# A hybrid attention/retention layer on one core: its modulation products in bursts of 16 k-tiles instead of 8, with half of their tiles in another pool

## The chip, the cores and the metric

The kernel runs on one core of a Trainium2 chip. The time is the device time of one execution in microseconds, as the median of several runs. The core has TensorE (PE for its matmuls, PEld for its weight loads), VectorE (DVE), ScalarE (ACT), GpSimd (POOL) and SyncE (SP), which issues most of the loads here.

## The reference, cut to what matters

One layer of a diffusion backbone: 256 latent tokens `x` and 256 context tokens `ctx`, width 4096, all in float32.

```python
mod = silu(c) @ ada_w + ada_b            # ada_w is 4096 x 12288
shift, scale, gate = split(mod, 3)
mod_c = silu(c_ctx) @ ada_w[:, :2*D] + ada_b[:2*D]
shift_c, scale_c = split(mod_c, 2)
h  = rms_norm(x, norm_w) * (1 + scale) + shift
hc = rms_norm(ctx, norm_w) * (1 + scale_c) + shift_c
proj = h @ w_in                          # 4096 x 14336; k and v of hc as well
...                                      # two groups of heads, gates
y = concat([o_d, o_r]) @ w_out
return x + gate * y
```

The change concerns the first lines: shift and scale of both token sets, that is two vectors (`c`, `c_ctx`) times the first 8192 columns of `ada_w`.

## The kernel before

The contraction of `h @ w_in` is cut into 32 k-tiles of 128 rows. A k-tile of `h` (its transposed tokens, 512 columns) can only be made when shift and scale of its 128 features are known, and these need all 4096 rows of the columns of `ada_w` that belong to it. So the kernel begins with a stage that alternates: the first `K1 = 20` k-tiles are worked off in chunks (`CHUNKS`: 1, 1, then nine times 2 k-tiles). For each chunk the adaLN products (class `Ada`) run over all 32 row tiles of `ada_w`, `finish` and `modulate` make the chunk's tiles `h`, and then six heads (`sheads`) multiply them with their columns of `w_in`: one `SUnit` a head, four row groups, three products each (a value is split in a high and a low part in `prep`), that is 24 matmuls of 512 columns where the chunk has two k-tiles. What is left of the 32 k-tiles is modulated later, on VectorE (`ada2_task`), beside other heads.

An adaLN product has a stationary operand of 32 columns, so four of them stand side by side in the array (`g = k % 4`); in float32 each is two passes, which the profile shows as two matmuls. `Ada.unit` runs one burst: `nk = 8` products, tied in order by `issue_after`, highest k first. A chunk has 32 products, so four bursts. `ada_to` calls `unit` so that a chunk's bursts are spread over the SUnits of the chunk before it (`LEAD`).

The tiles of `ada_w` have 4 KB a partition, 512 KB in all, loaded by two DMAs of 256 KB (`ada_load`, line 219). One holds two k-tiles of a chunk of width 2, or four of a chunk of width 1. They come from tag `adaw` with `ADAB = 6` buffers. `Ada.load` asks for the tiles of the next burst that is not asked for yet; it is called three times in the setup and once after each burst, so it stays three bursts ahead; a load waits until a buffer is free.

The pool `a4` has `SLOTS = 41` tiles of the same 4 KB a partition. It holds `x` and `ctx` at first (16), the transposed tokens `xr` (16, one for two k-tiles, free again when both are modulated), the tiles `h` (one a k-tile) and the sums of the heads `kvqg` (10 in this stage).

The weights of the heads go through `raw` (`RAWB = 3` buffers), are split on ACT (line 386) and DVE (line 387), four buffers each. Their DMAs (line 378) and those of `ada_w` are issued by SP, in one order: a DMA that has to wait holds those behind it. The order of the instructions on each engine, SP's issues among them, and the slots that tiles get, are fixed when the kernel is built, by a planner that goes by the order in the code and by its own estimate of when each thing is ready.

Of the kernel before, what the change touches and what calls it, by code (L numbers as in the profile page):

```python
# [10 lines left out]
F32 = mybir.dt.float32  # L11
# [7 lines left out]
P = 128  # L19
# [19 lines left out]
K1 = 20  # L39
# [4 lines left out]
ADAB = 6  # L44
# [38 lines left out]
def hybrid_kernel(es, tc, x, c, ctx, c_ctx, norm_w, ada_w, ada_b, w_in, q_norm_w, k_norm_w,  # L83
# [12 lines left out]
    a4 = es.enter_context(tc.tile_pool(name="a4", bufs=SLOTS, side="right"))  # L96
# [63 lines left out]
    adap = ada_cm.__enter__()  # L160
# [45 lines left out]

    ada_units = []
    for j, cn in enumerate(CHUNKS):
        nk = 8
        for k0 in range(0, KT, nk):  # L210
            ada_units.append((j, k0, nk))
    ada_end = [sum(1 for a in ada_units if a[0] <= j) for j in range(len(CHUNKS))]

    def ada_load(c0, cn, k0, name):

        n, m = cn * P, 4 // cn
        t = adap.tile([P, m, 2, n], F32, name=name, tag="adaw", bufs=ADAB)
        for s in range(2):
            nc.sync.dma_start(t[:, :, s], ada_w[k0 * P:(k0 + m) * P, s * D + c0 * P:s * D + c0 * P + n]  # L219
                              .rearrange("(k p) n -> p k n", p=P))  # L220
        return [t[:, k].rearrange("p s n -> p (s n)") for k in range(m)]

    class Ada:
# [5 lines left out]
        def load(self):  # L229

            p = self.pos + len(self.loaded)
            if p >= len(ada_units):
                return
            j, u0, nk = ada_units[p]
            tiles = []
            for k0 in range(u0, u0 + nk, 4 // CHUNKS[j]):
                tiles += ada_load(c0s[j], CHUNKS[j], k0, f"ada{j}_{k0}")
            self.loaded.append(tiles)
# [57 lines left out]
    def ada2_task():  # L296
# [4 lines left out]
        def load():  # L301
            if len(ahead) < len(work):
                j, k = work[len(ahead)]
                ahead.append(ada_load(c0s2[j], CHUNKS2[j], k, f"ada2_{j}_{k}")[0])
# [30 lines left out]
    ada = Ada()  # L335
    rbc = adap.tile([P, 512], F32, name="rbc")
    pr = aux_tile([P, 512], "pr")
    for half in range(2):
# [24 lines left out]
            nc.vector.tensor_scalar(dg, ident, rs[:, r:r + 1], None, op0=ALU.mult)  # L363
            nc.tensor.matmul(pr[:, rt * P:(rt + 1) * P], ones, dg, start=True, stop=True)
        ada.load()
    ada.load()
    nc.scalar.copy(rbc, pr)


# [720 lines left out]
```

## Time and profile before

| | |
|---|---|
| median of 3 runs | 2545.53 us (2541.44 to 2547.76) |
| the profiled execution | 2544.53 us |
| its span in the profile | 2542.7 us |
| PE busy | 2508.3 us of the span, mean granted clock 0.991 |
| moved by DMA | 563.70 MB |

The profile is of one execution; its own time is 1.8 us longer than the span. Times in its rows are from the start of the span. The profiled execution lies 1.0 us under the median of the runs.

### The profile page before, as it was taken

How to read it: one execution, taken by the hardware profiler on the slowest of the kernel's cores; microseconds unless marked ns; L12 is line 12 of the kernel's file. 1: busy time of each engine (PE TensorE's matmuls, PEld its weight loads, DVE VectorE, ACT ScalarE, POOL GpSimd, SP SyncE). 2: the span in 40 equal slices, each digit the busy share in tenths (PEclk: the TensorE clock that was granted, in tenths of full speed). 3: DMA queues.
4: the chain of work that ended last, by engine and by line, in shares of the span. 5: the costliest groups of instructions: out<-in, count | busy, mean ns of one | idle time of the engine just before them, and what ended most of it. 6: DMA issues, size and time to landing. Idle time of an engine off the chain costs nothing.

```text
span 2542.7 us, 36389 instructions
## 1 busy us (share of the span) xinstructions
PE 2508.3 (99%) x12634; PEld 2123.9 (84%) x12634; DVE 1726.4 (68%) x3026; ACT 992.2 (39%) x2017; POOL 44.6 (2%) x47
## 2 busy tenths in 40 slices
PE   7999999999999999999999999999999999999999
PEld 4566666888999997788888788899999999878887
DVE  5555555795897946777876887777777666655554
ACT  4222222222323233354445444554444444544443
POOL 0000000000000000000000000000000000000000
PEclk8999999999999999999999999999999999999999
DMA  9987978785686748766776676556666556676765
GB/s 315 291 284 243 292 230 292 244 269 176 198 274 192 252 105 278 235 219 196 239 241 202 201 238 227 185 178 199 198 207 203 169 152 189 197 238 207 229 208 175
DMA packets 497240, 563.70 MB, mean 222 GB/s; under 512 B 31696, under 2 KB 385296, under 8 KB 497056
## 3 DMA queue, kind: packets, MB, share of 16 engines
q1 hardware_dynamic: 480336, 526.57, 65.7%
q10 hardware_dynamic: 16720, 34.81, 4.0%
q8 instruction: 99, 1.62, 0.3%
q14 instruction: 85, 0.70, 0.1%
HBM read 538.17 MB, written 23.09 MB: 221 GB/s over the span
## 4 chain that ended last, share of the span: by engine, by line
PE 91%; DMA 5%; DVE 2%; SPq 1%; issue 1%; ACT 0%; DVEq 0%; ACTq 0%
PE psA L401 7%; PE psA L402 7%; PE psA L400 7%; PE psB L401 6%; PE psB L402 6%; PE psB L400 6%; PE psO L400 5%; PE psO L401 5%; PE psO L402 5%; PE pa L254 3%; DMA graw<-in_ada_w_dram 2%; DMA ada<-in_ada_w_dram 1%; DMA ostg<-o_dram 1%; SPq L219 1%; PE psA2s L551 1%; PE psA3s L551 1%
## 5 line engine op out<-in xcount | busy, mean ns | idle before, releaser
L386 ACT CAST whiB<-rawB 128x384 fp32r<-128x384 f32 x512 | 258.8, 512 | 455.5 <-PE psB L402 176.9
L387 DVE TENSOR_TENSOR wloB<-rawB,whiB 128x384 fp32r<-128x384 f32 x512 | 279.4, 553 | 170.7 <-ACT whiB L386 166.5
L386 ACT CAST whiA<-rawA 128x512 fp32r<-128x512 f32 x392 | 241.2, 620 | 380.9 <-PE psA L402 251.5
L401 PE MATMUL psA<-wloA,h 128*128 128x512 f32 x896 | 357.8, 399 | 2.6 <-DVE wloA L387 2.5
L402 PE MATMUL psA<-whiA,h 128*128 128x512 f32 x896 | 355.5, 397 | 0.0
L387 DVE TENSOR_TENSOR wloA<-rawA,whiA 128x512 fp32r<-128x512 f32 x392 | 268.3, 687 | 113.2 <-ACT whiA L386 112.3
L400 PE MATMUL psA<-whiA,h 128*128 128x512 f32 x896 | 319.2, 398 | 0.2 <-ACT whiA L386 0.2
L401 PE MATMUL psB<-wloB,h 128*128 128x384 f32 x896 | 303.4, 339 | 1.4 <-DVE wloB L387 1.3
L402 PE MATMUL psB<-whiB,h 128*128 128x384 f32 x896 | 301.7, 337 | 0.0
L387 DVE TENSOR_TENSOR wloO<-rawO,whiO 128x512 fp32r<-128x512 f32 x256 | 175.1, 691 | 154.9 <-ACT whiO L386 154.4
L400 PE MATMUL psB<-whiB,h 128*128 128x384 f32 x896 | 263.4, 339 | 1.9 <-ACT whiB L386 1.8
L386 ACT CAST whiO<-rawO 128x512 fp32r<-128x512 f32 x256 | 157.1, 620 | 198.1 <-PE psO L402 161.5
L320 DVE SCALAR_TENSOR_TENSOR acc<-ada,cT,acc 128x1024 f32<-128x1024 f32 x186 | 233.7, 1277 | 0.0
L934 DVE SCALAR_TENSOR_TENSOR gacc<-graw,cT,gacc 128x512 f32<-128x512 f32 x248 | 184.8, 745 | 49.1 <-DMA graw<-in_ada_w_dram 47.1
L401 PEld LDWEIGHTS psA<-wloA,h 128*128 128x128 f32 x896 | 168.7, 188 | 43.6 <-DVE wloA L387 5.1
L401 PE MATMUL psO<-wloO,o 128*128 128x512 f32 x512 | 203.2, 397 | 0.0
L402 PE MATMUL psO<-whiO,o 128*128 128x512 f32 x512 | 202.8, 396 | 0.0
L400 PEld LDWEIGHTS psA<-whiA,h 128*128 128x128 f32 x896 | 168.5, 189 | 40.0 <-ACT whiA L386 0.5
L402 PEld LDWEIGHTS psA<-whiA,h 128*128 128x128 f32 x896 | 168.7, 188 | 38.9
L401 PEld LDWEIGHTS psB<-wloB,h 128*128 128x128 f32 x896 | 168.5, 188 | 4.1 <-DVE wloB L387 3.6
L402 PEld LDWEIGHTS psB<-whiB,h 128*128 128x128 f32 x896 | 168.5, 188 | 0.3
L400 PEld LDWEIGHTS psB<-whiB,h 128*128 128x128 f32 x896 | 163.0, 188 | 3.9 <-ACT whiB L386 3.2
(395 smaller groups left out, 4250.4 us busy)
## 6 DMA issues: line engine op xcount, KB each, us to landing
ada<-in_ada_w_dram SPq DMA_DIRECT2D x512, 256.0 KB, 4.7
rawA<-in_w_in_dram SPq DMA_DIRECT2D x392, 256.0 KB, 3.4
rawB<-in_w_in_dram SPq DMA_DIRECT2D x256, 256.0 KB, 3.1
graw<-in_ada_w_dram SPq DMA_DIRECT2D x128, 512.0 KB, 5.0
rawO<-in_w_out_dram SPq DMA_DIRECT2D x128, 512.0 KB, 4.5
rawB<-in_w_in_dram SPq DMA_DIRECT2D x256, 128.0 KB, 2.8
p_dramA<-kvqgA ACTq DMA_DIRECT2D x16, 512.0 KB, 2.8
kvqgA<-p_dramA SPq DMA_DIRECT2D x16, 512.0 KB, 6.7
```

The lines of the kernel that those rows point to most:

```text
L219: nc.sync.dma_start(t[:, :, s], ada_w[k0 * P:(k0 + m) * P, s * D + c0 * P:s * D + c0 * P + n] .rearrange("(k p) n -> p k n", p=P))
L254: m = nc.tensor.matmul(self.pa[32 * g:32 * (g + 1), :], cpad[:, 2 * kt:2 * kt + 32], tiles[k], start=(u0 == 0 and i < 4), stop=(u0 + nk == ...
L320: nc.vector.scalar_tensor_tensor(acc[v], w, cv, acc[v], op0=ALU.mult, op1=ALU.add)
L386: nc.scalar.copy(hi, raw[:, k])
L387: nc.vector.tensor_tensor(lo, raw[:, k], hi.bitcast(F32), op=ALU.subtract)
L400: nc.tensor.matmul(pt[:, :ncol], a, hi, start=f, stop=False)
L401: nc.tensor.matmul(pt[:, :ncol], a, lo, start=False, stop=False)
L402: nc.tensor.matmul(pt[:, :ncol], b, hi, start=False, stop=e)
L551: nc.tensor.matmul(pt, a, hi, start=f, stop=False)
L934: nc.vector.scalar_tensor_tensor(acc, raw[:, k], cT[:, 0, kt:kt + 1], acc, op0=ALU.mult, op1=ALU.add)
```

## The change

Bursts have 16 products instead of 8, so a chunk has two of them instead of four. Of the tiles of `ada_w` that these bursts read (columns of the first 20 k-tiles) every second one, beginning with the first, is taken from `a4` instead of `adaw`; `ada2_task`'s stay in `adaw`. One of the three calls of `ada.load()` in the setup is removed, so the loads are asked for two bursts ahead, which is 32 k-tiles where it was 24.

```diff
     for j, cn in enumerate(CHUNKS):
-        nk = 8
+        nk = 16
         for k0 in range(0, KT, nk):
             ada_units.append((j, k0, nk))
...
+    flip = [0]
+
     def ada_load(c0, cn, k0, name):
 
         n, m = cn * P, 4 // cn
-        t = adap.tile([P, m, 2, n], F32, name=name, tag="adaw", bufs=ADAB)
+
+        flip[0] ^= 1
+        if c0 < K1 and flip[0]:
+            t = a4.tile([P, m, 2, n], F32, name=name, tag="a4")
+        else:
+            t = adap.tile([P, m, 2, n], F32, name=name, tag="adaw", bufs=ADAB)
         for s in range(2):
             nc.sync.dma_start(t[:, :, s], ...)
...
         ada.load()
-    ada.load()
     nc.scalar.copy(rbc, pr)
```

## Rows read from the trace of the kernel before

**Rows 1.** The page: span, busy time by engine, PE and clock in 40 slices.
```profile
span 2542.7 us, 36389 instructions
PE 2508.3 (99%) x12634; PEld 2123.9 (84%) x12634; DVE 1726.4 (68%) x3026; ACT 992.2 (39%) x2017; POOL 44.6 (2%) x47
PE   7999999999999999999999999999999999999999
PEclk8999999999999999999999999999999999999999
```
**Rows 2.** Windows by stage: engines' busy us, then granted clock, DMA share, GB/s.
```profile
0.00:48.00 48.00, 32.25 (x210) 21.23 (x214) 25.59 (x58) 25.23 (x72) 1.61 (x6) 0.83 1.02 316
48.00:130.00 82.00, 77.25 (x394) 47.48 (x387) 43.52 (x77) 20.11 (x37) 0.00 (x0) 0.91 0.96 296
130.00:452.00 322.00, 321.06 (x1591) 218.94 (x1590) 181.22 (x311) 72.27 (x126) 0.00 (x0) 1.00 0.83 267
492.00:2542.00 2050.00, 2037.75 (x10275) 1804.11 (x10273) 1451.41 (x2541) 863.66 (x1765) 42.96 (x41) 1.00 0.66 210
```
**Rows 3.** What PE waited for, 47 to 500 us, then 500 us to the end.
```profile
PE pa L254 <- DMA ada<-in_ada_w_dram: 4.2, 5, 3.1
PE psA0s L551 <- ACT h L292: 1.1, 1, 1.1
PE psA0s L551 <- DVE kvqgA L559: 0.3, 1, 0.3
...
PE psA L401 <- DVE wloA L387: 2.5, 3, 0.9
PE psB L400 <- ACT whiB L386: 1.8, 2, 1.1
```
**Rows 4.** Products and loads of tile ada, 48 to 130 us, then 130 to 452.
```profile
L254 PE MATMUL pa<-ada,cpad x176: 378/592/1063, 47.6 to 127.5; 128*32 128x512 f32 x112, 128*32 128x256 f32 x64
...
L254 PE MATMUL pa<-ada,cpad x464: 589/592/617, 134.0 to 440.4; 128*32 128x512 f32 x155
DMA to landing us min/median/max: 3.1/4.8/6.4
```
**Rows 5.** PE in order of time: a whole burst, then bursts in five pieces.
```profile
152.12 0.40 PE L553 MATMUL psP<-whiA5s,h 128*128 128x512 f32 x1
152.45 1.93 PE L254 MATMUL pa<-ada,cpad 128*32 128x512 f32 x16
154.30 0.50 PE L551 MATMUL psA0s<-whiA0s,h 128*128 128x512 f32 x1
154.64 0.40 PE L552 MATMUL psA0s<-wloA0s,h 128*128 128x512 f32 x1
154.88 0.40 PE L553 MATMUL psA0s<-whiA0s,h 128*128 128x512 f32 x1
...
186.97 1.06 PE L254 MATMUL pa<-ada,cpad 128*32 128x512 f32 x8
...
196.60 1.91 PE L254 MATMUL pa<-ada,cpad 128*32 128x512 f32 x12
...
199.10 1.05 PE L254 MATMUL pa<-ada,cpad 128*32 128x512 f32 x4
...
200.51 1.04 PE L254 MATMUL pa<-ada,cpad 128*32 128x512 f32 x2
...
205.18 1.06 PE L254 MATMUL pa<-ada,cpad 128*32 128x512 f32 x6
```
**Rows 6.** PE in order of time: the first matmul of the heads, and the longest wait.
```profile
49.48 0.80 PE L551 MATMUL psA0s<-whiA0s,h 128*128 128x512 f32 x1
...
80.64 3.75 PE L254 MATMUL pa<-ada,cpad 128*32 128x512 f32 x16 [3.10 <-DMA ada<-in_ada_w_dram]
```
**Rows 7.** SP's issues in order of time (start, us taken): setup, and later batches.
```profile
16.45 16.97 SPq L219 DMA_DIRECT2D ada<-in_ada_w_dram  x12
33.54 1.24 SPq L378 DMA_DIRECT2D rawA0s<-in_w_in_dram  x2
...
123.31 1.32 SPq L378 DMA_DIRECT2D rawA5s<-in_w_in_dram  x2
...
153.54 3.95 SPq L219 DMA_DIRECT2D ada<-in_ada_w_dram  x8
```
**Rows 8.** ACT in order of time: the split of that load of A5s.
```profile
139.72 1.32 ACT L386 CAST whiA5s<-rawA5s 128x512 fp32r<-128x512 f32 x2 [3.11 <-DVE kvqgA L559]
```
**Rows 9.** PE in order of time: the first products that read it.
```profile
143.92 0.86 PE L551 MATMUL psP<-whiA5s,h 128*128 128x512 f32 x3
```
**Rows 10.** What SP waited for, 0 to 460 us: in total, times, longest.
```profile
SPq L219 <- PE pa L254: 66.6, 41, 3.8
```

## The prediction

> **What bounds the kernel now.** I read the page first: PE is busy 2508.3 us of a span of 2542.7, and of its 40 slices only the first stands under nine tenths, and the clock is low there too [rows 1]. So there are two questions: what PE does with its time where it is full, and what it waits for at the start. The windows by stage answer the second. Up to 48 us the DMA engines run at a share of 1.02; from 48 to 130 us PE is idle for 4.75 us and the granted clock is 0.91, that is 0.18 of 82 us at the lower level (half speed), worth 7.4 us. Together at most 12 us are lost there, with the DMA share at 0.96. From 130 to 452 us, the rest of the stage that the change touches, PE is idle for 0.9 us at full clock, and the DMA share is 0.83 [rows 2]. The waits say the same: PE waited for tiles of ada five times, 4.2 us in all, of which one wait is 3.1 us, at 80 us [rows 3, 6]. From 492 us on PE is idle for 12 us of 2050 [rows 2], and its longest sums of waits are 2.5 and 1.8 us [rows 3]. So a microsecond saved on PE before 452 us comes out at the end nearly whole: what follows is issued as PE frees its buffers, with DMAs at 0.66.
>
> **What a burst costs.** In the order of time the last matmul before a whole burst starts at 152.12, the first behind it at 154.30 and the second at 154.64 [rows 5]. Two plain steps are 0.24 each (154.64 to 154.88), so the burst takes 2.52 - 0.48 = 2.04 us of PE for 16 passes. A piece of 8 passes stands in the record with 1.06 us against 1.93 for 16 [rows 5], so 8 passes more are 0.87 us. A burst of 32 passes is then 2.04 + 2 x 0.87 = 3.78 us, and two of 16 are 4.08: joining a pair saves 0.30 us. A reader sees why: the entry and the exit of a burst are paid once.
>
> **The terms.**
> *Whole bursts joined.* From 130 us on there are 464 passes, 29 bursts, and from 48 to 130 us 176 passes, 11 bursts [rows 4]. They become 14.5 and 5.5: 20 x 0.30 = 6.0 us. (The four of the first chunk run before 48 us, while DMAs set the pace: nothing.)
> *Broken bursts.* At 187 to 206 us two bursts run in five pieces of 8, 12, 4, 2 and 6 passes, with matmuls of the heads between them: 1.06 + 1.91 + 1.05 + 1.04 + 1.06 = 6.12 us against 3.86 for two whole ones, and three entries more at 0.12 (2.04 - 1.93), 2.6 us in all [rows 5]. The same pattern stands once more, at 318 to 338 us, so 5.2 us. The pieces come where the planner had no full burst of tiles in time: six buffers hold one and a half bursts of four tiles. Afterwards half of the tiles compete for the six and half for `a4`. I count its free slots from the code: 41 less 10 for the sums, 16 for `xr` and half a slot more for every `h` made, so 12 with six `h` and 6 with eighteen. A burst of the wide chunks wants four there and four of the six buffers: one and a half bursts fit, as now, but bursts of twice the length, with `a4` as wide as that late and twice as wide early. The bounds are 5.2 us (none broken) and a loss, since each break costs 0.87 (a third of 2.6); I take half, 2.6 us.
> *Waits for tiles beyond the start.* 4.2 - 3.1 = 1.1 us [rows 3]. A wait for the last of 16 can be as long as for the last of 8; I take 0.5, bounds 0 and 1.1.
> *The start.* Now all of chunk 0 (8 tiles, 16 DMAs) is asked for in the setup, and since `a4` has free slots, six of the eight tiles of chunk 1 can go out behind them, 12 DMAs, ahead of the heads' first weights, which come later in the code. Before, the sixth tile's DMA was the last that had a buffer, and the weights of A0s followed at 33.54 [rows 7]. The 12 issues there took 16.97 us, 1.41 each, as the queues were full; 28 of them end at 16.45 + 28 x 1.41 = 55.9 us. With a landing time of 4.8 us [rows 4] and a split of 1.3 us [rows 8] the weights reach PE at 62, where the first matmul stood at 49.48 [rows 6]: 12.5 us late. Against that, both bursts of chunk 1 are done by then, and the bytes that were fetched early are not fetched later. To reach the middle of chunk 3's products the kernel needs `x` and `ctx` 8.4 MB, 21.0 MB of `ada_w` and 4.2 MB of weights, 33.6 MB; by 126 us it had moved 48 x 316 + 78 x 296 = 38.3 MB [rows 2]. So DMAs could have been there some 16 us sooner with another order, and the 12 us of stalls are what can be gained; a late first matmul whose stalls return is the other end: 12.5 us less the bursts that fill it (four bursts of the narrow chunk, at about half of 2.04 each and with their breaks, near 6 us), a loss of 6. The stretch already has a DMA share of 0.96, so I stay near the row and take a gain of 2.0 us, bounds -6 and +9 (three of the twelve are clock that returns with any wait).
> *No cost.* The number of DMAs, bytes, products and passes is the same. The longer burst holds the heads' matmuls up by 1.7 us more at a time; VectorE is busy 181 of 322 us there and ACT 72 [rows 2], so what they owe PE is ready behind it. If that cover were gone, it would show as PE waiting for line 386 or 387.
> *Sum:* 6.0 + 2.6 + 0.5 + 2.0 = 11.1 us against the profiled execution's 2544.5, so 2533.4 us; the median of the runs is 1.0 us higher than that execution, which I leave in the range.
>
> **A rule that speaks against it.** SP's loads are one order. A batch of eight issues takes 3.95 us, 0.49 each, when nothing blocks it [rows 7]; a burst of 16 frees eight tiles at once, so 16 issues, 7.9 us, and 4.2 MB, at 267 GB/s [rows 2] 15.7 us. A weight load behind it lands after that and one landing time, 15.7 + 4.8 [rows 4] = 20.5 us. The weights of A5s were issued at 123.31, split at 139.72 and multiplied at 143.92 [rows 7, 8, 9]: 16.4 and 20.6 us ahead. The Trainium skill ("DMA: Bandwidth & Descriptors", section on queues, rings and completion order) says that on each DMA engine descriptors are consumed in ring order, so a load cannot pass the batch issued ahead of it. By that rule weights come just at the edge, with nothing to spare; by the row of SP's waits, 41 waits for PE of up to 3.8 us [rows 10] cost PE nothing, so the lead has some give.
>
> **Rivals.**
> *1, slower: weights stuck behind a batch.* As worked out, 20.5 us against a lead of 20.6. It decides from there on: each microsecond more, at each of the 18 bursts of the wide chunks, is 18 us. The 11.1 us are gone at 0.6 us a burst; at 1.5 us the time is 2544.5 - 11.1 + 27 = 2560. For it: the doubled batch. Against it: freed slots of `a4` and `adaw` come at different times, so batches should be smaller than 16. It would show as ACT waiting for raw loads and PE behind it.
> *2, no change: bursts break.* If 20 bursts break once each at 0.87, that is 17.4 us instead of the 5.2 of now; joining, 6.0, and the start, 2.0, leave 2544.5 + 12.2 - 8.5 = 2548; with ten breaks it is 2540. For it: it happens now at two places, and `a4` gets short late. Against it: 25 of 29 bursts are whole now with 1.5 bursts of buffers.
> *3, smaller: the tiles `h` find no slot.* In the late chunks `a4` has 6 to 8 free slots, and loads two bursts ahead want eight. If they take them all, the next two `h` wait for a burst to free some, and PE for `h`: two or three chunks at 2 to 4 us, and 2533.4 + 9 = 2542. Against it: `finish` comes first in the code.
> *4, the start goes the wrong way:* -6 instead of +2, so 2541.
>
> **Chances.** The forecast (2524 to 2537) 0.60, rival 1 0.09, rival 2 0.16, rivals 3 and 4 0.15. Some 0.3% of this time, 7.6 us, is what a measurement can tell from no change, so faster means under 2537.9. The forecast lies under that; of rivals 2 to 4 about a third of the weight does, so faster 0.69; rival 1 and a part of 2 are slower than 2553, 0.09; the rest 0.22. The range: best all terms at their upper bounds, 6.0 + 5.2 + 1.1 + 9 = 21 (2523); at the other end joining alone with the start lost, 6.0 - 6 = 0 (2544.5). It leaves out rival 1 and the worse half of 2, and the tail below.
>
> **What would show it.** Bursts of 32 passes with 3.67 us in the record (1.93 + 2 x 0.87) and few pieces; the last product of the six heads near 481 us where it was 492; no PE wait for lines 386 or 387 before 450 us; the first matmul of the heads later than 49.5 us but a granted clock over 0.91 from there to 130 us. Wrong it would be with ACT or PE waiting for raw loads (rival 1), more than ten extra pieces (2), PE waiting for `h` past 300 us (3), or more than 12 us lost from 48 to 130 us (4).

## The result, and the profile after

The changed kernel takes 2557.07 us (median of 6 runs, 2554.58 to 2562.83), the kernel before 2543.80 beside it (6 runs, 2540.41 to 2547.76). The ratio is 1.0055 [1.0040, 1.0071]: slower by half a per cent, where I had forecast 2533.4 and given 0.09 to a slowdown. The profiled execution after is 2555.34 us, 10.8 us above the profiled one of before, and that difference can be placed. Lines below `ada_load` have moved: the products are L261 now (L254 before), their loads L226 (L219), the loads of the heads' weights L384 (L378), the splits L392 and L393 (L386, L387), the heads' matmuls L557 to L559 (L551 to L553).

The page of after answers to [rows 1]; little is to be seen there but the first two digits of PE, 6 and 8 where they were 7 and 9.
```profile
span 2553.5 us, 36288 instructions
PE 2507.6 (98%) x12634; PEld 2125.0 (83%) x12634; DVE 1722.7 (67%) x3026; ACT 991.3 (39%) x2017; POOL 44.6 (2%) x47
PE   6899999999999999999999999999999999999999
```
The windows of the stage, with the columns of [rows 2]:
```profile
48.00:130.00 82.00, 71.44 (x378) 45.64 (x382) 45.33 (x79) 21.54 (x40) 0.00 (x0) 0.94 1.00 312
130.00:452.00 322.00, 319.83 (x1573) 214.27 (x1562) 174.02 (x301) 70.43 (x122) 0.00 (x0) 1.00 0.82 259
```
From 48 to 130 us PE is idle for 10.6 us where it was 4.75, with a granted clock of 0.94 where it was 0.91. From 130 to 452 us it is nearly as busy as before, for 319.83 of 322 us, and still it gets less done: 1573 matmuls where there were 1591. So the first stretch shows waits, and the second shows PE's time spent on something that costs more. How far the kernel has come is told by the matmuls of the six heads: their last one of chunk 2 starts at 156.3 us where it started at 152.1, and the last one of the stage at 500.9 where it was 492.3. That is 4.2 us lost by chunk 2 and 4.4 more by the end of the stage; the span has 2.2 more, lost after that.

What PE waited for, 28 to 520 us (in total, times, longest; [rows 3] of before begin later, at 47 us):
```profile
PE pa L261 <- DMA ada<-in_ada_w_dram: 8.2, 2, 6.0
PE psA0s L557 <- ACT h L299: 5.9, 3, 4.4
...
PE psA0s L557 <- ACT whiA0s L392: 2.2, 1, 2.2
PE psA3s L557 <- ACT whiA3s L392: 2.2, 1, 2.2
```
The two last rows are new: PE waits for splits of the heads' weights. They come back in the order of time on PE, which also has a broken burst and the one wait for tiles of ada beyond the start:
```profile
51.74 0.80 PE L557 MATMUL psA0s<-whiA0s,h 128*128 128x512 f32 x1 [4.40 <-ACT h L299]
...
77.66 0.74 PE L557 MATMUL psA0s<-whiA0s,h 128*128 128x512 f32 x2 [2.25 <-ACT whiA0s L392]
...
98.05 1.34 PE L557 MATMUL psA3s<-whiA3s,h 128*128 128x512 f32 x4 [2.23 <-ACT whiA3s L392]
...
174.12 0.40 PE L559 MATMUL psA2s<-whiA2s,h 128*128 128x512 f32 x1
174.44 2.77 PE L261 MATMUL pa<-ada,cpad 128*32 128x512 f32 x20
177.14 0.50 PE L557 MATMUL psA2s<-whiA2s,h 128*128 128x512 f32 x1
177.48 0.40 PE L558 MATMUL psA2s<-wloA2s,h 128*128 128x512 f32 x1
...
178.41 0.40 PE L559 MATMUL psA2s<-whiA2s,h 128*128 128x512 f32 x1
178.74 1.06 PE L261 MATMUL pa<-ada,cpad 128*32 128x512 f32 x6
...
182.73 1.06 PE L261 MATMUL pa<-ada,cpad 128*32 128x512 f32 x6
...
441.67 2.77 PE L261 MATMUL pa<-ada,cpad 128*32 128x512 f32 x20 [2.17 <-DMA ada<-in_ada_w_dram]
```
The burst of 32 passes stands there as 20, 6 and 6. Priced as the prediction priced bursts, the first piece takes PE 2.89 us (174.12 to 177.48, less two plain steps) and the others 1.18 each: 5.25 us, and PE waits for nothing between them. The built order of PE tells how often that happens. These are the stretches of products without another matmul between them, 352 products in all:
```
before  8 8 16 8 3 5 8 2 6 8 8 8 8 8 8 8 8 8 8 8 8 4 6 2 1 3 8 8 8 8 8 8 8 8 8 8
        4 6 2 1 3 8 8 8 8 8 8 8 8 8 8   (51 pieces)
after   4 28 16 14 2 16 16 16 11 1 4 16 10 3 3 16 9 3 4 10 6 9 3 4 16 9 1 3 3 16
        9 7 11 5 9 3 4 16 10 3 3   (41 pieces)
```
The first five of after, and the first nine of before, are the narrow chunks. Of the 18 bursts of the wide chunks 10 are broken after, at 18 places; of 36 before, 4 were.

The new waits have their cause on SP, whose issues are (start, us taken; [rows 7] are those of before):
```profile
17.45 26.11 SPq L226 DMA_DIRECT2D ada<-in_ada_w_dram  x24
43.68 1.51 SPq L384 DMA_DIRECT2D rawA0s<-in_w_in_dram  x2
...
60.32 10.29 SPq L226 DMA_DIRECT2D ada<-in_ada_w_dram  x16
71.00 1.06 SPq L384 DMA_DIRECT2D rawA0s<-in_w_in_dram  x2
...
75.44 15.46 SPq L226 DMA_DIRECT2D ada<-in_ada_w_dram  x24
91.33 1.06 SPq L384 DMA_DIRECT2D rawA3s<-in_w_in_dram  x2
```
and the chain of work from 66 us on joins one of them to its wait:
```profile
66.20 5.51 DMA ada<-in_ada_w_dram
...
71.72 5.19 DMA rawA0s<-in_w_in_dram
...
76.99 0.63 ACT whiA0s L392
...
77.66 0.74 PE psA0s L557 x2
```
Sixteen issues take SP from 60.32 to 70.61; the weights of A0s come behind them, land 5.2 us later, are split, and PE, which works in a fixed order, stands for 2.25 us. The batch of 24 ahead of A3s does the same at 98 us.

### The profile page after: what moved, and what is told of

Read it like the earlier page. It is cut to its first block, busy times and chain, and to the rows that moved or that the text cites. A ratio compares the mean times of both kernels' runs of the same rounds, so it can differ in the third digit from the quotient of the medians.

```text
span 2553.5 us, 36288 instructions
## 1 busy us (share of the span) xinstructions
PE 2507.6 (98%) x12634; PEld 2125.0 (83%) x12634; DVE 1722.7 (67%) x3026; ACT 991.3 (39%) x2017; POOL 44.6 (2%) x47
## 4 chain that ended last, share of the span: by engine, by line
PE 89%; DMA 6%; DVE 2%; SPq 1%; issue 1%; ACT 0%; DVEq 0%; ACTq 0%
PE psA L407 7%; PE psA L408 7%; PE psA L406 7%; PE psB L407 6%; PE psB L408 6%; PE psB L406 6%; PE psO L407 5%; PE psO L408 5%; PE psO L406 5%; PE pa L261 3%; DMA ostg<-o_dram 1%; DMA ada<-in_ada_w_dram 1%; DMA graw<-in_ada_w_dram 1%; SPq L226 1%; PE psA2s L557 1%; PE psA6p L406 1%
## 5 line engine op out<-in xcount | busy, mean ns | idle before, releaser
L392 ACT CAST whiB<-rawB 128x384 fp32r<-128x384 f32 x512 | 258.6, 512 | 451.0 <-PE psB L408 172.2
L393 DVE TENSOR_TENSOR wloB<-rawB,whiB 128x384 fp32r<-128x384 f32 x512 | 278.9, 554 | 164.9 <-ACT whiB L392 162.4
L392 ACT CAST whiA<-rawA 128x512 fp32r<-128x512 f32 x392 | 241.4, 620 | 380.6 <-PE psA L408 250.3
L393 DVE TENSOR_TENSOR wloA<-rawA,whiA 128x512 fp32r<-128x512 f32 x392 | 268.1, 687 | 112.5 <-ACT whiA L392 111.6
L393 DVE TENSOR_TENSOR wloO<-rawO,whiO 128x512 fp32r<-128x512 f32 x256 | 175.1, 691 | 153.4 <-ACT whiO L392 153.1
L392 ACT CAST whiO<-rawO 128x512 fp32r<-128x512 f32 x256 | 157.2, 621 | 197.1 <-PE psO L408 150.8
```

The costliest lines, as they stand in the source:

```text
L392: nc.scalar.copy(hi, raw[:, k])
L393: nc.vector.tensor_tensor(lo, raw[:, k], hi.bitcast(F32), op=ALU.subtract)
```

## The experiments

Two theories of the loss between them, and a third that the prediction had held. *Broken bursts*: the tiles lie ready earlier, so the planner begins a burst ahead of heads' matmuls that stand before it in the code, and then lets these in between its products; `issue_after` ties the order of products to one another, and nothing keeps other work out. *Tile supply*: bursts break because their tiles come late. *Weights behind batches*: rival 1 of the prediction, at the start. Each run is told with its ratio to the kernel before, measured on the same chip (medians of that kernel 2541.3 to 2542.3 us), and is compared with the changed kernel, which was measured beside 2543.80, through these ratios.

**whole16.** The changed kernel, with the products after a burst's first put ahead of other ready work.
```diff
-                with nullcontext() if prev is None else tc.issue_after(prev):
+                with nullcontext() if prev is None else tc.issue_after(prev), \
+                     nullcontext() if prev is None else tc.high_priority():
```


> The changed kernel, with one thing more: inside a burst every product after the first gets a higher planning priority than the heads' matmuls, so that a burst once begun is finished. In the planned order of TensorE the 41 pieces become 22. From the pieces of the changed kernel's trace (entry 0.33 us, 0.86 us for every four products begun) the bursts after the first chunk cost 88.1 us of TensorE in the changed kernel and 72.0 here. Theory 1 (the planner, not the tiles, breaks the bursts, and breaking costs what joining was to save): 16 us less than the changed kernel, near 2541 us. Theory 2 (bursts break because tiles are not there): the pieces turn into idle time of TensorE waiting for tiles of ada, and the time stays within 4 us of 2557.

2539.26 us, ratio 0.9989 [0.9980, 0.9997], that is 0.66% under the changed kernel. All bursts but the first are whole (4 28 and then twenty of 16). PE in order of time, at the same place in the code as the broken one above:
```profile
168.65 0.40 PE L559 MATMUL psA2s<-whiA2s,h 128*128 128x512 f32 x1
168.98 3.64 PE L261 MATMUL pa<-ada,cpad 128*32 128x512 f32 x32
172.55 0.50 PE L557 MATMUL psA2s<-whiA2s,h 128*128 128x512 f32 x1
172.88 0.40 PE L558 MATMUL psA2s<-wloA2s,h 128*128 128x512 f32 x1
```
A whole one costs 4.23 - 0.47 = 3.76 us, against 5.25 in three pieces. What PE waited for, 28 to 520 us:
```profile
PE pa L261 <- DMA ada<-in_ada_w_dram: 8.8, 3, 6.6
...
PE psA0s L557 <- ACT whiA0s L392: 3.6, 2, 2.9
PE psA3s L557 <- ACT whiA3s L392: 2.3, 1, 2.3
```
If late tiles had broken the bursts, those kept whole would wait for them instead. The first row holds 6.6 us at the start and leaves 2.2 us in two waits, where the changed kernel had 2.17 in one. So tile supply isn't what broke them. The waits for weights at the start stay, as they should.

**whole8.** The same line in the kernel before, with its bursts of 8.

> The kernel before, bursts of 8, with the same priority inside a burst; 51 planned pieces become 43. By the same costs 85.5 us of bursts become 78.6. Theory 1: 7 us less than before, near 2537 us. Theory 2: no change from before, 2544 us, with waits for ada tiles in place of the pieces.

2537.54 us, 0.9986 [0.9977, 0.9994]. With bursts kept whole the two lengths differ by nothing that these runs can tell (0.9989 and 0.9986). Here the theory of tile supply does find its place: with six buffers and bursts kept whole, waits for tiles take the place of breaks: beyond 130 us PE waits for them 4.2 us in six, where before had 0.9 in three.
```profile
PE pa L254 <- DMA ada<-in_ada_w_dram: 4.2, 6, 1.5
```

**pool8.** The changed kernel with bursts of 8 and the third early load back, so of the change only the alternating pools are left.
```diff
-        nk = 16
+        nk = 8
...
         ada.load()
+    ada.load()
```


> The kernel before with only the tiles changed: every second one from the large pool, bursts of 8, three calls of load in the setup. If the longer burst alone is what loses time, this stays at 2544 us. If the tiles' pool (bursts can begin earlier than their place in the code, and get broken by matmuls that stand before them) is what does it, the bursts cost 100.4 us instead of 85.5 by the 56 planned pieces: 15 us more than before, near 2559 us, with the start as late as in the changed kernel on top (5 us).

2558.69 us, 1.0072 [1.0058, 1.0086]: this part alone costs as much as the whole change. PE's order has 56 pieces:
```
pool8   4 28 16 4 8 4 10 8 6 8 18 8 6 8 9 9 3 3 11 3 2 1 11 4 6 8 2 1 11 4 6 2 1
        2 10 9 2 11 3 2 1 11 4 6 8 2 1 11 4 6 2 1 2 10 9 2   (56 pieces)
```
With more buffers bursts break more often; that they break because they begin earlier is what the next run tests.

**in_place16.** The changed kernel, without the priority; a burst's first product may not go ahead of the heads' matmul that stands before it in the code.
```diff
-            prev = None
+            prev = last_mm[0]      # the heads' matmul emitted last
```


> The changed kernel, without any priority; instead the first product of a burst is tied behind the last matmul of the heads that stands before it in the code. If bursts break because the planner begins them ahead of matmuls that stand before them and then lets those in, 22 whole pieces result without a priority, and the time is near that of whole bursts (2539 us), plus what the later modulation costs at the chunks' ends. If TensorE then waits for the tiles h of the next chunk, 1 to 3 us for each of nine chunks, 2550 to 2565.

2542.35 us, 1.0002 [0.9992, 1.0012], with the bursts whole again (22 stretches, as in whole16), though nothing keeps other work out of them. So it is the early start that breaks them, as the theory has it. But the start in place has a price of its own; the waits of PE show it, 28 to 520 us:
```profile
PE psA0s L559 <- ACT h L301: 10.1, 8, 4.1
```
The changed kernel had 5.9 us in 3 there. That fits products which are done later and make the next chunk's `h` later. A burst that starts early and is not interrupted did better (whole16, 0.9989), though the two intervals touch.

**weights_first16.** The changed kernel with the loads of the six heads' weights put ahead of other ready loads on SP.
```diff
-            m = nc.sync.dma_start(raw[:, :, o:o + wd], ...)
+            with tc.high_priority() if "s" in name else nullcontext():
+                m = nc.sync.dma_start(raw[:, :, o:o + wd], ...)
```


> The changed kernel, with the loads of the heads' weights given a higher planning priority than the loads of ada_w as long as the bursts run. The bursts are as broken as in the changed kernel (40 planned pieces, 87.8 us). If the waits for the heads' weights behind batches of ada_w loads (at 77 and 98 us of the changed kernel's trace, 4.5 us idle and about 5 us at the lower clock) are part of the loss, the time falls by 5 to 9 us, to 2548 to 2552; if the bytes set the pace of the start, TensorE waits for tiles of ada there instead, and the time stays at 2557.

2547.62 us, 1.0032 [1.0019, 1.0044], 0.23% under the changed kernel, with bursts as broken as there; the two intervals just touch (1.0040 to 1.0044). On SP the second chunk's weights of A0s go out at 62.49 us, where they went at 71.00:
```profile
57.99 4.40 SPq L226 DMA_DIRECT2D ada<-in_ada_w_dram  x8
62.49 1.30 SPq L385 DMA_DIRECT2D rawA0s<-in_w_in_dram  x2
```
and PE's waits for splits are gone from the list, 28 to 520 us:
```profile
PE pa L261 <- DMA ada<-in_ada_w_dram: 9.7, 3, 6.6
PE psA0s L558 <- ACT h L299: 6.7, 3, 4.4
```

**whole_wfirst16.** Both additions in the changed kernel.

> The changed kernel with both additions: whole bursts and the heads' weight loads ahead of the ada_w loads. If the two losses are separate (pieces, and weights behind batches at the start), the gains add: the priority of the weights took 9.5 us off the changed kernel, so some 8 us less than whole bursts alone, near 2531 us, with no wait of TensorE for the split of weights left from 48 to 130 us. If they overlap (the same stalls counted twice), it stays at 2537 to 2540.

2534.28 us, 0.9974 [0.9964, 0.9983]: 0.81% under the changed kernel, where the two apart sum to 0.89. The two causes add up within the intervals. With both taken away it stands 0.26% below the kernel before, where I had forecast 0.44% (2533.4 of 2544.5).

**whole_wfirst8.** Both additions in the kernel before, with its six buffers.

> The kernel before (bursts of 8, six buffers) with the same two additions. The kernel before has no wait for weights at its start, so theory 1 expects what whole bursts of 8 alone gave, 2536 to 2538 us; joining bursts to 16 is then worth the difference to the run with 16, 6.6 us by the pieces (78.6 against 72.0). If the start's order matters for it as well, it falls to near 2530 and joining is worth nothing.

2547.71 us, 1.0025 [1.0016, 1.0035], slower; a miss. Its partner is whole8 (0.9986), from which it differs in the order of the loads alone. The windows from 48 to 130 us tell why, whole8's first, then this run's, with its two long waits for tiles below:
```profile
48.00:130.00 82.00, 76.36 (x405) 48.74 (x398) 44.50 (x79) 20.45 (x39) 0.00 (x0) 0.95 0.96 305
48.00:130.00 82.00, 73.33 (x361) 45.32 (x354) 40.79 (x72) 18.46 (x35) 0.00 (x0) 0.86 0.86 269
...
82.97 3.03 PE L254 MATMUL pa<-ada,cpad 128*32 128x512 f32 x16 [2.84 <-DMA ada<-in_ada_w_dram]
103.52 3.25 PE L254 MATMUL pa<-ada,cpad 128*32 128x512 f32 x16 [3.07 <-DMA ada<-in_ada_w_dram]
```
whole8 has the first of the two, at 80.06 us, and only 0.69 us at the place of the second. With weights always ahead and few buffers for the tiles of ada, these come late: the DMA share falls to 0.86 from 0.96, PE is idle for 8.7 us where it was 5.6, and the clock is lower by 0.09 of 82 us, 7.4 us. What is put ahead must be paid for with room for what it passes.

**whole_pool8.** pool8 with whole bursts.

> Bursts of 8 with every second tile from the large pool and three loads ahead, and whole bursts. The bursts cost 78.3 us by the planned pieces, as whole bursts of 8 without the pool (78.6). If the pool's only harm was the broken bursts, 2537 us like those; if the loads that it lets go early also hold the first weights up, some 5 us more, 2542.

2538.85 us, 0.9986 [0.9976, 0.9995]: the alternating pools cost nothing once bursts stay whole (beyond 130 us all are; some before that are not). No wait of PE for tiles of ada stands beyond 130 us, where whole8 had 4.2 us of them. The total shows no gain of it yet: at the start PE waits for splits of weights, which whole8 does not, 28 to 520 us:
```profile
PE psA3s L558 <- ACT whiA3s L393: 3.7, 2, 2.9
PE psA4s L558 <- ACT whiA4s L393: 1.9, 1, 1.9
```

**start_first16.** The changed kernel with the weights of two heads prepared ahead of chunk 1's tiles, which wait for their issue (`tc.issue_after(last_raw[0])`).

> The changed kernel, with only the start reordered: the first two heads' weights are asked for before the ada_w tiles of chunk 1, whose loads are tied behind them. The bursts stay broken (42 planned pieces, 89.7 us against 88.1). If the changed kernel's start loses its time to the first weights (first matmul of the heads at 51.74 us, behind a load issued at 43.7), the first matmul comes near 48 us and the time falls by 3 to 5 us less the 1.6 of the pieces: 2553 to 2556. If the bytes set the pace, the wait moves to the tiles of chunk 1, and the time is 2557 to 2560.

2553.01 us, 1.0042 [1.0028, 1.0055]. The first matmul of the heads comes at 46.03 us, 5.7 sooner, and the gain is given back within chunk 0, whose last heads' matmul starts 2.0 us later than in the changed kernel:
```profile
PE psP L558 <- ACT whiA5s L393: 5.1, 1, 5.1
```
By the end of chunk 2 the profiled execution is 5.0 us ahead again (151.3 against 156.3); it is the fastest of its five, and by the medians the gain is 0.13%, with intervals that overlap widely.

**all_fixes16.** whole_wfirst16 with that start.

> All three additions: whole bursts of 16, weights ahead of ada_w, the start reordered. If the start's order is a loss of its own, 3 us under whole bursts with weights first (2534.3): near 2531 us. If not, 2534.

2538.39 us, 0.9986 [0.9976, 0.9995], worse than without it; a miss too. In the profiled execution, the slowest of its eleven, PE waits 5.7 us for a split of A0s:
```profile
PE psA0s L559 <- ACT whiA0s L394: 5.7, 1, 5.7
```
The start that the prediction argued about is bound by loads, and moving one ahead makes another late. Why this wait comes out longer than all that was gained wasn't tried further.

**whole_wfirst_pool8.** Bursts of 8, three early loads, alternating pools, whole bursts, weights first: whole_wfirst16 without the joining.

> Bursts of 8, whole, with every second tile from the large pool and the weights ahead: against the run with bursts of 16 it shows what joining itself is worth. By the planned pieces 80.1 us against 72.3, so 2534.3 + 7.8 = 2542. But in the run whole_pool8 neighbouring bursts of 8 often ran back to back, and from 130 us on its pieces cost 1 us more than bursts of 16; by that 2535 to 2537. If the pool is also what cures the slow run of bursts of 8 with weights first and six buffers (2547.7), it is well under that.

2531.14 us, 0.9961 [0.9949, 0.9974], the fastest of all by its median, faster than both kernels. Its windows, 48 to 130 us and 130 to 452:
```profile
48.00:130.00 82.00, 78.12 (x404) 48.23 (x405) 47.43 (x82) 23.16 (x43) 0.00 (x0) 0.98 1.07 337
130.00:452.00 322.00, 322.00 (x1616) 225.19 (x1615) 185.83 (x324) 74.40 (x131) 0.00 (x0) 1.00 0.82 261
```
PE is idle for 3.9 us in the first of them, at a clock of 0.98, and not at all in the second. Against whole_wfirst8 only the alternating pools are added, and they are worth 0.64%: with room for the tiles, weights can go first. What SP waited for from 48 to 130 us, whole_wfirst8 first, shows the room: it hardly waits any more for PE to free a buffer of ada.
```profile
SPq L219 <- PE pa L254: 15.4, 7, 3.6
...
SPq L226 <- PE pa L261: 1.0, 3, 0.4
```
Joining brings no gain on top that these runs can tell (0.9974 [0.9964, 0.9983] with it).

Side by side, with the start of the stage's last heads' matmul, and what the pieces beyond 130 us cost PE, each priced as above from the time of its neighbours, waits ahead of it included. The passes differ because 130 us falls at another place in each kernel's work. Both columns come from one execution each: whole16's is the fastest of its eleven (2535.94 us), whole8's the slowest (2542.21), so these two are compared by their medians:

| kernel | ratio | stage ends, us | pieces; passes; us |
|---|---|---|---|
| before | 1 | 492.3 | 35; 464; 66.5 |
| after | 1.0055 | 500.9 | 32; 458; 70.8 |
| pool8 | 1.0072 | 504.4 | 43; 448; 78.3 |
| whole16 | 0.9989 | 482.2 | 14; 448; 55.3 |
| whole8 | 0.9986 | 488.7 | 29; 464; 65.3 |
| whole_pool8 | 0.9986 | 484.3 | 23; 448; 56.3 |
| in_place16 | 1.0002 | 489.2 | |
| weights_first16 | 1.0032 | 495.5 | 30; 462; 70.5 |
| whole_wfirst16 | 0.9974 | 481.4 | 14; 448; 56.1 |
| whole_wfirst8 | 1.0025 | 498.0 | |
| start_first16 | 1.0042 | 496.3 | |
| all_fixes16 | 0.9986 | 486.2 | |
| whole_wfirst_pool8 | 0.9961 | 478.5 | |

The last column says what each kernel paid. Before: 29 bursts at 2.04 are 59.2 us, the two groups of five pieces cost 5.5 more (2.73 each), and three waits for tiles with two late starts make up the 1.8 that are left. After: 458 passes at 3.76 for 32 are 53.8, the wait at 441.67 is 2.2, and breaks make up 14.8. For the kernels with the pools it also answers why joining brings so little: neighbouring bursts of 8 run back to back when their tiles lie ready (23 pieces in whole_pool8 where there are 28 bursts), at 56.3 us; the 14 joined ones cost 52.7, and 2.6, most of it waits for tiles, make that 55.3. Why whole8, whose bursts do not run together, is as fast as whole16 by its median is not shown.

## Why the prediction was wrong

**What held.** The bound: a microsecond of PE before 452 us comes out at the end. The stage of whole16 ends 18.7 us before that of after, and its span is 19.4 us shorter. The price of a joined burst, 3.78 us, measured 3.76.

**The step that failed: "Broken bursts", a gain of 2.6 us.** I put the pieces of before down to tiles that were not there in time, so that more room for them had to be a gain and a break could only come from a shortage. For the kernel before that reading has something in it: kept whole, its bursts wait for tiles (whole8), and the alternating pools end these waits (whole_pool8). But I missed the second way to a broken burst, and it has the other sign: more buffers let a burst begin ahead of its place, and then heads' matmuls come in between. pool8 alone is 1.0072, and in_place16, which only forbids the early start, has whole bursts with the same buffers. Breaks beyond 130 us cost 14.8 us where they were 5.5: the term was +9.3, not -2.6. The bounds that I had set were "none broken" on one side and a loss without a figure on the other, and the range left that loss out. (2.04 - 1.93 is 0.11 and not 0.12 there, which leaves the 2.6 as it is.)

**"Whole bursts joined", 6.0 us.** The price was right, 59.2 - 53.8 = 5.4 us beyond 130 us (0.7 of it because six passes fewer stand there). With the breaks, +9.3, and 0.4 more of waits that makes the 4.3 by which the table's two sums differ, and 4.4 is what was lost between chunk 2 and the end of the stage.

**"The start", a gain of 2.0 us with bounds of -6 and +9.** By the end of chunk 2 the changed kernel is 4.2 us behind: a loss, inside the bounds. Broken bursts have a part in it, which these runs don't separate: in the profiled executions whole16 ends chunk 2 5.5 us before the changed kernel (150.8) and weights_first16 5.1 (151.2). The first matmul of the heads came at 51.74 us and not at 62: 24 issues went ahead of the weights and not 28, and they took 26.11 us, 1.09 each and not 1.41. The wait there is put down to `h`, but the chain of work shows the weights behind it, since ACT splits those of A0s to A2s before it makes that `h`:
```profile
46.66 3.91 DMA rawA2s<-in_w_in_dram
50.66 0.62 ACT whiA2s L392
51.27 0.42 ACT h L299
51.74 0.80 PE psA0s L557
```
The rest came where I hadn't looked, in the second and third chunk, behind batches of 16 and 24 issues. PE's idle time grew by 5.8 us from 48 to 130 us, and the clock gave back 0.03 of 82, 2.5 us.

**Rival 1 happened at the start, not in each chunk.** I asked for batches of 16 and argued that slots come free at different times; at the start they are free from the beginning, and the batches were 16 and 24. Beyond 130 us no wait for splits stands among the waits, so what it priced for the 18 bursts of the wide chunks stayed away there. weights_first16 takes the waits away and 0.23% of the time, 5.9 us. The Trainium skill ("DMA: Bandwidth & Descriptors", section on queues, rings and completion order) has descriptors consumed in ring order on each engine; the trace agrees: the last of the sixteen, issued at 70.24, lands at 76.17 us, and A0s, issued behind it at 71.72, at 76.91. That a load "cannot pass" is the prediction's own step, since by the same section a later one may finish its write first. The 5.2 us are no more than other weights take there (3.9 to 7.2 us before 140 us). A0s was late because SP first issued the sixteen, until 70.61.

**Rival 2 happened too, and decided, by another cause.** Its reason was that `a4` gets short; it was room that broke the bursts. I gave it 2548 with 20 breaks, at 0.87 each. The burst shown paid 0.75 for each of its breaks ((5.25 - 3.76) / 2), and after has 18 in the wide chunks. With a loss of 4.2 in place of the start's gain of 2.0 it becomes 2554, near the 2555.34 of the profiled execution. I had given the two 0.25 together, each alone. For a slowdown I had 0.09, said to hold rival 1 and a part of 2, and rival 1 alone has 0.09.

**Rival 3 and the waits for tiles.** A shortage of slots for `h` did not show: the longest wait for it, 4.40 us, is the one at 51.74, and beyond 100 us the two there sum to 1.5. The waits for tiles, for which I had taken a gain of 0.5, are 2.2 us beyond 130 us where they were 0.9.

**What stays open.** The 2.2 us that the span loses after the end of the stage, which lie within what the 13 profiled executions differ by there (2048.0 to 2056.9 us from the end of the stage to the end of the span); and the 2.5 us by which the medians differ more (13.3) than the two profiled executions (10.8). Bursts of 16 with all tiles in `adaw` were not run: one such burst of a wide chunk holds eight tiles, and there are six buffers. Nor was the removed third early load run by itself.

## What to carry to other kernels

A tie of order between instructions is not a tie of place: where a planner fills an engine, more buffers let filler work begin earlier and be cut into pieces, each with its entry and exit; so count the pieces before counting on fewer of them, and give a burst that has begun priority to its end. Whether late data broke it shows when it is kept whole: then a wait takes the place of the break, or nothing does. Where one queue loads for two consumers, put what is due first ahead, but only together with buffers for what it passes: with whole bursts of 8 the order alone was a loss here (1.0025 where it was 0.9986), the buffers alone changed nothing (0.9986), and both together were the fastest (0.9961).

## What was unexpected in the hardware

A piece of 6 passes and a piece of 8 cost PE the same: 1.18 us for 6 (178.41 to 180.06, less two plain steps), and in [rows 5] the records of pieces of 2, 4, 6 and 8 passes are 1.04, 1.05, 1.06 and 1.06 us. Four products stand side by side in the array, and the prices above come out as 0.87 us for each group of four begun and some 0.3 us a piece on top (1.18 for one group, 2.04 for two, 2.89 for three, 3.76 for four). So a burst cut into 10, 3 and 3 products pays for five groups and three entries, where the whole one pays for four and one.

That entry and exit cost anything by themselves has a rule: the Trainium skill ("TensorEngine Tiling (Array Packing)", section on key properties) says that a change of the tiling mode drains the engine. The rows fit it without showing a drain: the step into a burst (168.65 to 168.98) and the one behind its first follower (172.55 to 172.88) are 0.33 us each where plain ones are 0.24. The first follower starts 0.07 us before the burst's record ends (172.55 against 168.98 + 3.64), but these ends are modelled. The page has no price for it.
